# Dense gate tiles from two fp32r products with the gate values in two parts

## The chip, the cores and the metric

The kernel runs on one core of a Trainium2 chip. The metric is the device time of one execution in microseconds (us). Engines are called PE (matrix products; PEld is its weight load), DVE (vector), ACT (scalar, activations), POOL (GpSimd, here mostly the issuer of gather DMAs) and SP (the queue that issues most DMAs).

## The reference, cut to what matters

Two layers of a trunk over 512 latent tokens (and 256 context tokens in the first layer) with 1024 channels. Each layer ends in PEER retrieval: a token has 8 heads, each head picks 16 of 16384 experts by product keys, and an expert is a pair of rows of two tables u and v.

```python
top_s, pos = lax.top_k(cand, PEER_TOPK)
eidx = jnp.take_along_axis(cidx, pos, axis=-1)          # expert = i * 128 + j
gate = jax.nn.softmax(top_s, axis=-1)
act = jax.nn.gelu(jnp.einsum('nd,nhkd->nhk', hb, u_tab[eidx]).astype(F32), approximate=False)
w = (gate * act).astype(hb.dtype)
return jnp.einsum('nhk,nhkd->nd', w, v_tab[eidx])
```

So a token has 128 chosen experts (i, j), each with a gate value.

## The kernel before, in words

Tokens lie in tiles of 128. Most tiles are "dense": for them the kernel computes u times the token for all 16384 experts, with Gelu, multiplies by a 128x128 matrix of gates of each token (zero but for the chosen experts) and multiplies the product with v. Layer 0 has four dense tiles (n = 512 columns) and two gathered ones, layer 1 has three (n = 384) and one. A gathered tile fetches its rows of u and v with indirect DMAs (POOL, L667), and DVE works each row off with one 128x1024 instruction (L671, L675).

A layer's PEER has a first stage over 128 chunks of u (`u_chunk`): SP loads a chunk (`c_raw`, 512 KB), ACT casts it to fp32r (`c_hi`, L297), DVE subtracts to get the rest (`c_lo`, L298), and PE makes 24 products into `ups` (8 blocks of channels, three products each: c_hi with the high part of the tokens `opah`, c_hi with the low part `opal`, c_lo with `opah`; in layer 1 the names are `opch` and `opcl`). ACT's Gelu (`at`, L938) empties `ups`. `c_hi` and `c_lo` have two buffers, so those of a chunk wait for PE's end of the chunk two before. A second stage multiplies the gated values with v (`res`).

The gates are made beside the first stage. `select(t)` finds a tile's experts and leaves, transposed so that a partition is one of a token's 128 choices and a column a token, the row numbers -i and the gate values in `ijT` (L804), and the column numbers j as bf16 in `jT`. `build(t)` then goes over the 128 tokens, four at a time (W8), which makes 32 builds a tile, 224 in all (128 in layer 0, 96 in layer 1). For one build:

- ACT makes `o1`: per token |iota - i| (L820, four instructions of 128 columns), then Relu(1 - that) over all four (L821): a one where the row matches.
- DVE makes `oe`, a bf16 one where the column number matches (L824), and multiplies it by the gate values into `o2` (L825). `oe` lies as columns by tokens, tokens innermost; `o2` is written as tokens by columns, so DVE's writes go with a stride of 512 bytes.
- PE multiplies o1 and o2 of each token, a plain fp32 product of 128 columns (`gps`). One fp32 product shows as two MATMUL and two LDWEIGHTS records, so a build is 8 records.
- ACT copies `gps` to `stage` (L830), which goes to DRAM every fourth build.

`back` decides what is queued behind each chunk: it keeps clocks for PE, DVE and DMA from the table COST (a build is entered with 1.03 on DVE and .85 on PE), issues a share of the builds after each chunk and fills DVE with rows of the gathered tiles while its clock is behind. That table is the same before and after. Instructions on an engine run in the order in which they were issued by the framework; a wait holds up what stands behind it.

## Time and profile before

| What | Before |
|---|---|
| time, median of 3 runs | 3865.34 us (3862.36 to 3866.61) |
| the profiled execution | 3875.51 us, span 3873.7 us |
| PE, PEld busy in the span | 95%, 82% |
| DVE, ACT, POOL busy | 80%, 47%, 46% |
| mean granted clock of PE | 0.979 of 2.4 GHz |

The shares are means over stages with different limits. Builds run from 804.7 us to 3280.8 us in two stretches, about 780 to 1380 us (layer 0) and 2880 to 3290 us (layer 1). Matmul records overlap their neighbours, so the pace of PE is read from starts, not from durations.

### The profile page before, as it was taken

How to read it: one execution, taken by the hardware profiler on the slowest of the kernel's cores; microseconds unless marked ns; L12 is line 12 of the kernel's file. 1: busy time of each engine (PE TensorE's matmuls, PEld its weight loads, DVE VectorE, ACT ScalarE, POOL GpSimd, SP SyncE). 2: the span in 40 equal slices, each digit the busy share in tenths (PEclk: the TensorE clock that was granted, in tenths of full speed). 3: DMA queues.
4: the chain of work that ended last, by engine and by line, in shares of the span. 5: the costliest groups of instructions: out<-in, count | busy, mean ns of one | idle time of the engine just before them, and what ended most of it. 6: DMA issues, size and time to landing. Idle time of an engine off the chain costs nothing. (4 is left out here: it accounts for less than half of the span.)

```text
span 3873.7 us, 56946 instructions
## 1 busy us (share of the span) xinstructions
PE 3669.3 (95%) x20375; PEld 3169.8 (82%) x20375; DVE 3109.4 (80%) x6128; ACT 1839.1 (47%) x3241; POOL 1785.7 (46%) x1225
## 2 busy tenths in 40 slices
PE   7789999999999999999999899899999999999998
PEld 5567778787888778888887888789999999887877
DVE  4876899999999968877776715688999996677778
ACT  4243322377788932322224434533348999333332
POOL 4300155456556557777771203203433331577773
PEclk9899999999999999999999999899999999999999
DMA  5225589899999999989994440157989897888885
GB/s 230 87 90 202 208 320 329 309 332 357 359 347 358 371 327 357 339 321 335 336 330 139 139 135 4 66 177 266 312 296 335 322 326 272 276 312 321 320 320 198
DMA packets 377147, 1043.98 MB, mean 270 GB/s; under 512 B 32288, under 2 KB 171936, under 8 KB 346656
## 3 DMA queue, kind: packets, MB, share of 16 engines
q1 hardware_dynamic: 262960, 619.56, 44.2%
q0 software_dynamic: 113760, 420.53, 30.4%
q8 instruction: 160, 2.62, 0.3%
q14 instruction: 123, 1.01, 0.1%
q10 hardware_dynamic: 144, 0.26, 0.0%
HBM read 915.98 MB, written 124.26 MB: 269 GB/s over the span
## 5 line engine op out<-in xcount | busy, mean ns | idle before, releaser
L667 POOL DMA_INDIRECT g_row<-in_peer_u_dram,g_idx x384 | 562.7, 1465 | 670.7 <-DVE g_row L671 296.4
L667 POOL DMA_INDIRECT g_row<-in_peer_v_dram,g_idx x384 | 573.4, 1493 | 283.3 <-DVE g_acc L675 157.1
L1075 POOL TENSOR_TENSOR w<-ag,gg 128x512 f32<-128x512 f32 (+1 forms) x256 | 487.8, 1906 | 379.6 <-DVE w_lo L298 286.3
L298 DVE TENSOR_TENSOR v_lo<-v_raw,v_hi 128x1024 fp32r<-128x1024 f32 x256 | 392.4, 1533 | 286.9 <-ACT v_hi L297 286.9
L297 ACT CAST c_hi<-c_raw 128x1024 fp32r<-128x1024 f32 x304 | 318.2, 1047 | 618.4 <-PE ups L69 516.6
L297 ACT CAST v_hi<-v_raw 128x1024 fp32r<-128x1024 f32 x256 | 269.5, 1053 | 701.3 <-PE res L69 411.1
L69 PE MATMUL res<-v_hi,w_hi 128*128 128x512 f32 x1792 | 555.4, 390 | 10.3 <-ACT w_hi L297 10.2
L69 PE MATMUL res<-v_lo,w_hi 128*128 128x512 f32 x1792 | 554.6, 390 | 1.2
L69 PE MATMUL res<-v_hi,w_lo 128*128 128x512 f32 x1792 | 553.5, 389 | 0.0
L675 DVE SCALAR_TENSOR_TENSOR g_acc<-g_row,g_act,g_acc 128x1024 f32<-128x1024 f32 x381 | 520.1, 1365 | 4.4 <-DMA g_row<-in_peer_v_dram,g_idx 1.8
L298 DVE TENSOR_TENSOR c_lo<-c_raw,c_hi 128x1024 fp32r<-128x1024 f32 x304 | 372.4, 1225 | 144.7 <-ACT c_hi L297 144.2
L671 DVE SCALAR_TENSOR_TENSOR g_row<-g_row,g_h 128x1024 f32<-128x1024 f32 x384 | 471.7, 1245 | 12.6 <-DMA g_row<-in_peer_u_dram,g_idx 12.6
L69 PE MATMUL ups<-opah,c_lo 128*128 128x512 f32 x1152 | 453.8, 395 | 14.0 <-DVE c_lo L298 13.7
L69 PE MATMUL ups<-opah,c_hi 128*128 128x512 f32 x1152 | 461.6, 401 | 3.9 <-ACT c_hi L297 3.9
L69 PE MATMUL ups<-opal,c_hi 128*128 128x512 f32 x1152 | 453.2, 393 | 0.0
L69 PEld LDWEIGHTS res<-v_hi,w_hi 128*128 128x128 f32 x1792 | 336.0, 188 | 83.8 <-ACT w_hi L297 14.8
L69 PEld LDWEIGHTS res<-v_lo,w_hi 128*128 128x128 f32 x1792 | 335.9, 188 | 74.8 <-DVE v_lo L298 5.8
L69 PE MATMUL ups<-opch,c_hi 128*128 128x384 f32 x1152 | 393.5, 342 | 1.8 <-ACT c_hi L297 1.8
L69 PEld LDWEIGHTS res<-v_hi,w_lo 128*128 128x128 f32 x1792 | 335.9, 188 | 70.8 <-DVE w_lo L298 1.7
L69 PE MATMUL ups<-opch,c_lo 128*128 128x384 f32 x1152 | 388.1, 337 | 3.1 <-DVE c_lo L298 3.1
L69 PE MATMUL ups<-opcl,c_hi 128*128 128x384 f32 x1152 | 387.0, 336 | 0.0
L820 ACT ACTIVATE o<-iota,ijT 128x128 f32<-128x128 f32 x896 | 290.5, 399 | 0.0
(487 smaller groups left out, 6738.5 us busy)
## 6 DMA issues: line engine op xcount, KB each, us to landing
c_raw<-in_uT_dram SPq DMA_DIRECT2D x256, 512.0 KB, 6.5
v_raw<-in_peer_v_dram SPq DMA_DIRECT2D x128, 1024.0 KB, 6.9
G_d<-stage SPq DMA_DIRECT2D x56, 1024.0 KB, 7.9
c_raw<-in_peer_wq_dram SPq DMA_DIRECT2D x64, 512.0 KB, 4.9
gg<-G_d SPq DMA_DIRECT2D x64, 512.0 KB, 9.5
A_d<-at SPq DMA_DIRECT2D x120, 256.0 KB, 6.6
ag<-A_d SPq DMA_DIRECT2D x30, 1024.0 KB, 10.1
gg<-G_d SPq DMA_DIRECT2D x64, 384.0 KB, 7.9
```

The costliest lines, as they stand in the source:

```text
L69: self.last = self.engine.matmul(*args, **kw)
L297: copied[0] = S.copy(hi, src)
L298: return V.tensor_tensor(lo, src, hi.bitcast(F32), op=OP.subtract)
L667: G.indirect_dma_start(out=row, out_offset=None, in_=a[f"peer_{'uv'[tab]}{l}"], in_offset=bass.IndirectOffsetOnAxis(ap=idx[i][:, s:s + 1], ...
L671: V.scalar_tensor_tensor(row, row, 1.0, h, op0=OP.mult, op1=OP.mult, accum_out=w)
L675: V.scalar_tensor_tensor(acc, row, w, acc, op0=OP.mult, op1=OP.add)
L820: S.activation(o1[:, i], iota, AF.Abs, bias=tr[:, 0, n0 + i:n0 + i + 1])
L1075: G.tensor_tensor(w.rearrange("p (t m) -> p t m", m=TG), ag[:, i], gg[:, :, (c + i) % GG, :], op=OP.mult)
```

## The change

The gate values are split into a high part rounded to fp32r (kept in the third row of `ijT`) and a low part `gl`. `oe` is multiplied by each part, so `o2` becomes `o2h` and `o2l`, both fp32r, both kept as columns by tokens, which DVE writes without a stride. PE makes two fp32r products per token, o1 with o2h and o1 with o2l, added up in PSUM; it reads a token's 128 columns of o2 with a stride of 16 bytes. ACT writes |iota - i| into a tile `of` of its own and Relu of it into `o1`. The buffers change: `o1` two to one, `oe` two to one, `o2h` two, `o2l` one, `of` one.

```diff
-                S.copy(tr, pt)
+                S.copy(tr[:, :2], pt[:, :2])
                 jb = wp.tile([P, P], BF16, name="jT", bufs=2)
                 S.copy(jb, pt[:, 1])
-                chosen[t] = tr, jb
+                gl = wp.tile([P, P], F32R, name="gl", bufs=2)
+                split(tr[:, 2].bitcast(F32R), gl, pt[:, 2])
+                chosen[t] = tr, jb, (tr[:, 2], gl.bitcast(F32))
...
-                tr, jb = chosen.pop(t)
+                tr, jb, gh = chosen.pop(t)
...
-                        o1 = wp.tile([P, W8, P], F32, name="o1", bufs=2)
-                        o2 = wp.tile([P, W8, P], F32, name="o2", bufs=2)
+                        sh, nb = [P, P, W8], slice(n0, n0 + W8)
+                        o1 = wp.tile([P, W8, P], F32R, name="o1", bufs=1)
+                        o2 = [wp.tile(sh, F32R, name=f"o2{y}", bufs=b_) for y, b_ in (("h", 2), ("l", 1))]
+                        of = wp.tile([P, W8, P], F32, name="of", bufs=1)
                         for i in range(W8):
-                            S.activation(o1[:, i], iota, AF.Abs, bias=tr[:, 0, n0 + i:n0 + i + 1])
-                        S.activation(o1, o1, AF.Relu, bias=1.0, scale=-1.0)
-                        sh, nb = [P, P, W8], slice(n0, n0 + W8)
-                        oe = wp.tile(sh, BF16, name="oe", bufs=2)
+                            S.activation(of[:, i], iota, AF.Abs, bias=tr[:, 0, n0 + i:n0 + i + 1])
+                        S.activation(o1, of, AF.Relu, bias=1.0, scale=-1.0)
+                        oe = wp.tile(sh, BF16, name="oe", bufs=1)
                         V.tensor_tensor(oe, iotar, jb[:, nb].unsqueeze(1).to_broadcast(sh), op=OP.is_equal)
-                        V.tensor_tensor(o2.rearrange("p n c -> p c n"), oe, tr[:, 2, nb].unsqueeze(1).to_broadcast(sh),
-                                        op=OP.mult)
+                        for y in range(2):
+                            V.tensor_tensor(o2[y], oe, gh[y][:, nb].unsqueeze(1).to_broadcast(sh), op=OP.mult)
                         pg = pp.tile([P, W8, P], F32, name="gps", tag="misc", bufs=4)
                         for i in range(W8):
-                            PE.matmul(pg[:, i], o1[:, i], o2[:, i], start=True, stop=True)
+                            for y in range(2):
+                                PE.matmul(pg[:, i], o1[:, i], o2[y][:, :, i], start=y == 0, stop=y == 1)
```

With the single buffers the framework also issues builds in another place. Numbers at a name tell one buffer or one build from another; the rows are from layer 0, where two builds follow one chunk.

On PE, before, the two builds (10564, 10584) stand together between the last product of chunk 10526 and the first of chunk 10602:

```order
L69 MATMUL ups_10526<-opah0_1455,c_lo_10523 128x512
L69 MATMUL gps_10564<-o2_10555,o1_10554 128x128
L69 MATMUL gps_10564<-o2_10555,o1_10554 128x128 x3
L69 MATMUL gps_10584<-o2_10575,o1_10574 128x128
L69 MATMUL gps_10584<-o2_10575,o1_10574 128x128 x3
L69 MATMUL ups_10602<-opah0_1455,c_hi_10598 128x512
```

On PE, after, at a like place (the last of the eight products of build 10451, then chunk 10501, then build 10476):

```order
L69 MATMUL gps_10451<-o2l_10440,o1_10438 128x128
L69 MATMUL ups_10501<-opah0_1455,c_hi_10497 128x512
L69 MATMUL ups_10501<-opal0_1457,c_hi_10497 128x512
L69 MATMUL ups_10501<-opah0_1455,c_lo_10498 128x512
L69 MATMUL ups_10501<-opah0_1455,c_hi_10497 128x512
L69 MATMUL ups_10501<-opal0_1457,c_hi_10497 128x512
L69 MATMUL ups_10501<-opah0_1455,c_lo_10498 128x512
L69 MATMUL gps_10476<-o2h_10464,o1_10463 128x128
L69 MATMUL gps_10476<-o2l_10465,o1_10463 128x128
```

The second build of a pair has moved six products (seven in layer 1) into the next chunk; no two builds stand together any more. Before there are 43 such pairs in layer 0 and 21 in layer 1; 32 are among the first 96 builds of layer 0 and 10 among the first 66 of layer 1, and as many of these builds stand early in a chunk after.

On ACT, before, for the same pair (`at` is the Gelu of a chunk, `stage` the copy of a finished build):

```order
L297 CAST c_hi_10663<-c_raw_10661 128x1024
L938 ACTIVATE at_10551<-ups_10526 128x512
L830 COPY stage_10490<-gps_10564 128x4x128
L820 ACTIVATE o1_10634<-iota_62,ijT_9746 128x128
L830 COPY stage_10490<-gps_10584 128x4x128
```

On ACT, after, for builds 10451 (first) and 10476 (second) behind chunk 10410:

```order
L297 CAST c_hi_10566<-c_raw_10564 128x1024
L942 ACTIVATE at_10435<-ups_10410 128x512
L834 COPY stage_10317<-gps_10451 128x4x128
L825 ACTIVATE o1_10463<-of_10466 128x512
L824 ACTIVATE of_10536<-iota_62,ijT_10172 128x128
L824 ACTIVATE of_10536<-iota_62,ijT_10172 128x128 x3
L834 COPY stage_10317<-gps_10476 128x4x128
```

Before, the `o1` of both builds was made ahead of these rows; after, the Relu that makes the second build's `o1` stands behind the copy of the first build.

On DVE, before, the two multiplications of a pair stand behind one `c_lo`:

```order
L298 TENSOR_TENSOR c_lo_10599<-c_raw_10596,c_hi_10598 128x1024
L825 TENSOR_TENSOR o2_10555<-oe_10561,ijT_9746 128x128x4
L825 TENSOR_TENSOR o2_10575<-oe_10581,ijT_9746 128x128x4
```

On DVE, after, from the `c_lo` of chunk 10570 on:

```order
L298 TENSOR_TENSOR c_lo_10567<-c_raw_10564,c_hi_10566 128x1024
L829 TENSOR_TENSOR o2l_10465<-oe_10472,gl_10176 128x512
L753 MAX topd_10384<-candd_10387 128x8
L827 TENSOR_TENSOR oe_10542<-iotar_2702,jT_10174 128x512
L754 MAX_INDEX posd_10385<-topd_10384,candd_10387 128x8
L829 TENSOR_TENSOR o2h_10534<-oe_10542,ijT_10172 128x512
L755 MATCH_REPLACE c2d_10623<-topd_10384,candd_10387 128x96
L675 SCALAR_TENSOR_TENSOR g_acc_86<-g_row_10650,g_act_2681,g_acc_86 128x1024
L829 TENSOR_TENSOR o2l_10535<-oe_10542,gl_10176 128x512
```

Each build now has two multiplications on DVE, and the one that writes `o2l` waits for PE's products of the build before; in its place on the queue it mostly stands behind a `c_lo`.

## Rows read from the trace of the kernel before

**Rows 1.** Windows: stretch, length, then busy PE, PEld, DVE, ACT, POOL (instructions), clock, DMA, GB/s.
```profile
780.00:1260.00 480.00, 459.49 (x2368) 386.75 (x2366) 474.97 (x863) 380.90 (x750) 286.64 (x175) 0.99 0.96 351
1260.00:1380.00 120.00, 110.87 (x604) 93.53 (x605) 107.33 (x165) 102.70 (x215) 65.85 (x45) 1.00 0.99 372
2880.00:3180.00 300.00, 298.57 (x1903) 297.63 (x1901) 286.21 (x570) 268.58 (x527) 108.15 (x76) 1.00 0.90 322
3180.00:3290.00 110.00, 102.45 (x656) 98.21 (x655) 78.22 (x92) 104.66 (x224) 23.48 (x16) 1.00 0.77 278
```
**Rows 2.** Waits in 780 to 1260 us: who waited for whom, total us, times, longest.
```profile
ACT c_hi L297 <- PE ups L69: 67.0, 40, 4.4
...
PEld gps L69 <- ACT o L821: 14.8, 10, 2.9
```
**Rows 3.** DVE's groups in 780 to 1380 us: busy us, mean ns | idle before.
```profile
L825 DVE TENSOR_TENSOR o<-oe,ijT 128x512 f32<-128x512 bf16 x128 | 137.0, 1086 | 2.1 <-PE gps L69 2.1
L298 DVE TENSOR_TENSOR c_lo<-c_raw,c_hi 128x1024 fp32r<-128x1024 f32 x81 | 98.7, 1218 | 8.1 <-ACT c_hi L297 8.1
L824 DVE TENSOR_TENSOR oe<-iotar,jT 128x512 bf16<-128x512 bf16 x128 | 51.2, 416 | 0.0
```
**Rows 4.** Chain of work in 3030 to 3090 us: start us, us, what.
```profile
3036.20 0.89 PE gps L69 x8
3037.09 4.17 PE ups L69 x24
```
**Rows 5.** DVE over the whole span: 512 fp32 elements of two SBUF tiles into fp32r.
```profile
L298 DVE TENSOR_TENSOR w_lo<-w,w_hi 128x512 fp32r<-128x512 f32 x128 | 87.3, 682 | 0.0
```
**Rows 6.** Line L825 alone by stretch: length, busy us (instructions), clock, DMA, GB/s.
```profile
780.00:1260.00 480.00, 102.66 (x96) 0.99 0.96 351
...
2880.00:3180.00 300.00, 70.55 (x66) 1.00 0.90 322
```
**Rows 7.** PE's timeline from 2350.3 us: start us, us, what.
```profile
2350.29 1.45 PE L69 MATMUL po<-gkv,apT 128*128 128x64 f32 x12
2351.58 1.11 PE L69 MATMUL mlps<-vx,kw 128*128 128x129 f32 x8
```
**Rows 8.** Weight loads over the whole span, by form.
```profile
L69 PEld LDWEIGHTS gps<-o,o 128*128 128x128 f32 x1792 | 223.5, 191 | 55.4 <-ACT o L821 39.1 <-ACT o L820 3.3 <-issue 3.0
L69 PEld LDWEIGHTS ups<-opah,c_hi 128*128 128x128 f32 x1152 | 218.7, 190 | 48.6 <-ACT c_hi L297 7.3
...
L69 PEld LDWEIGHTS modp<-modw,scT 128*2 128x2 f32 x1024 | 27.4, 94 | 19.6 <-issue 10.2 <-DMA modw<-in_mod_w_dram 3.6 <-DVE sib L721 0.8
```
**Rows 9.** PE's timeline in layer 1's projection, fp32r products of 256 columns.
```profile
2292.66 0.28 PE L69 MATMUL tps<-t_hi,opbh 128*128 128x256 f32 x1
2292.78 0.28 PE L69 MATMUL tps<-t_lo,opbh 128*128 128x256 f32 x1
```
**Rows 10.** PE's timeline around one build in layer 0.
```profile
1006.21 0.39 PE L69 MATMUL ups<-opal,c_hi 128*128 128x512 f32 x1
1006.44 0.40 PE L69 MATMUL ups<-opah,c_lo 128*128 128x512 f32 x1
1006.67 1.06 PE L69 MATMUL gps<-o,o 128*128 128x128 f32 x8
1007.48 0.48 PE L69 MATMUL ups<-opah,c_hi 128*128 128x512 f32 x1
```
**Rows 11.** ACT's timeline behind the same chunk.
```profile
1006.69 1.03 ACT L297 CAST c_hi<-c_raw 128x1024 fp32r<-128x1024 f32 x1
1007.63 0.59 ACT L938 ACTIVATE at<-ups 128x512 f32<-128x512 f32 x1
1008.11 1.06 ACT L830 COPY stage<-gps 128x512 f32<-128x512 f32 x1
1008.97 1.27 ACT L820 ACTIVATE o<-iota,ijT 128x128 f32<-128x128 f32 x4
1010.27 0.63 ACT L821 ACTIVATE o<-o 128x512 f32<-128x512 f32 x1
```

## The prediction

> **What bounds the kernel now.** I read the busy times by stretch first, since the page's means mix stages. In the first part of layer 0's builds (780 to 1260 us) DVE is busy 474.97 of 480 us, PE 459.49 and ACT 380.90 [rows 1]: DVE has 5 us left and PE 20.5. The next 120 us, where builds come three to a chunk, have no engine full: PE 110.87, DVE 107.33, ACT 102.70. In layer 1, from 2880 to 3180 us, PE is busy 298.57 of 300 us and DVE 286.21; then ACT takes over (104.66 of 110 us) while DVE falls to 78.22 [rows 1]. Then the waits: in the full stretch of layer 0, PE's idle time before builds is mostly put down to ACT's Relu (14.8 us), and ACT itself waits 67 us for PE to give the chunk buffers back [rows 2]. DVE waits hardly at all: 2.1 us before o2, 8.1 us before c_lo over 600 us [rows 3]. So in layer 0 DVE works without a pause and PE just keeps up; in layer 1 the chain of work is PE alone, 4.17 us for a chunk and 0.89 us for a build [rows 4], with DVE 14 us short of full.
>
> **DVE, the term that counts.** One strided multiplication of 1086 ns goes [rows 3], two unstrided ones come. The nearest row is w_lo: 512 elements of two SBUF tiles, at least one of them fp32, into fp32r, 682 ns [rows 5]. A build then costs 2 x 0.682 - 1.086 = +0.278 us on DVE. Bounds: the new form is not in the trace. If the stride was not what made the old one slow, both cost 1.086, +1.09 us a build; if both ran like the bf16 comparison oe, 416 ns [rows 3], the build saves 0.25 us. I take 0.682, because there an fp32 operand is read as here, while oe is bf16 throughout.
> Layer 0, full stretch: 96 builds [rows 6] x 0.278 = 26.7 us on an engine with 5 us of idle time. I put +27 there, since the idle time did not close before either. The other 32 builds add 8.9 us where DVE has 12.7 us to spare [rows 1]: nothing. If that cover fails, it costs those 8.9 us.
> Layer 1: 66 builds [rows 6] x 0.278 = 18.3 us, DVE to 304.6 of 300 us: it becomes the bound by 4.6 us. The last 30 builds fall where DVE has 32 us to spare: nothing.
> The splitting of the gates is once a tile, seven times, each three instructions of 128 columns where one of 384 is cut to 256: an estimate of 0.3 us each on DVE (less than oe's 0.416 for four times the columns), 1 us on the path.
>
> **PE.** A build was 8 records of fp32, and is 8 of fp32r: two products for a token instead of the two passes of one. What can a product of 128 columns cost? Twelve records of po with only 64 columns take 2351.58 - 2350.29 = 1.29 us, 0.108 us each [rows 7]; eight of gps with 128 columns take 0.89, 0.111 each [rows 4]. Half the columns do not make it faster, so the weight load of 128 columns sets the pace, not the stream. That load is the same for fp32r: 190 ns in ups against 191 in gps, where one of 2 columns takes 94 [rows 8]. And the new products load o1 twice per token, as before. So a record stays at 0.108 at the least; the nearest fp32r row, 256 columns, is 0.12 apart [rows 9], the upper end if the strided read is free. I take 0.117 x 8 = 0.94, +0.05 us a build: hidden behind DVE in layer 0, 66 x 0.05 = 3 us in layer 1. If the stride costs at most the time of a second column each, the stream of 128 columns lasts like one of 256, which is again the 0.12. The bound above: four column times each, as long as the 512 column products, 0.23 us [rows 10], 1.84 a build, +0.95.
> The Trainium skill speaks against this strided read: SBUF — State Buffer, "Door 1" with its note on cachelines, has 16-byte lines, full rate from two hits in a line on, and a penalty for each access that goes to a new line; here every column is a new line. No row of this case shows a strided moving operand, so by that rule the sum lies between my 0.94 and the 1.84 above; it is the second rival's ground.
> The Trainium skill has a rule on the other side too: TensorE: Matmul & The Clock Gate, "Back-to-back issue gap", gives about 81 ns for a pair of weight load and product of 128 columns. The trace disagrees for four-byte weights: 0.108 us even with 64 columns [rows 7]. By that page of the Trainium skill a build would be 0.65 us, an estimate, and layer 1's stretch would lose 16 us of PE work, none of which counts while DVE has 304.6 us to do in it.
>
> **Order and single buffers.** The waits added: Relu into o1 and the multiplication into o2l now wait for PE's previous build. Behind the first stand ACT's next Abs, c_hi and Gelu; behind the second DVE's gather rows and c_lo. Where one build follows a chunk, the previous build is 0.89 + 4.17 us or more ahead and o2l stands behind a c_lo of 1.22 us [rows 3, 4], so nothing is late. Where two follow, the second has moved six products into the next chunk, and its Relu stands behind c_hi, Gelu and the copy of the first. Counted from the chunk's end (by starts, as records overlap): c_hi to copy 1.42, copy to next 0.86, Relu 0.63 [rows 11], so o1 is there 2.9 us after. PE is there after 0.81 for the first build and 6 x 0.23 = 1.4 [rows 10], 2.2 us after. PE stands 0.7 us per pair: 32 pairs in layer 0's full stretch, 22 us; 10 in layer 1's, 7 us (there 7 products of 0.174 against a shorter Gelu, the same 0.7). In layer 0 most of this lies beside the time that PE lacks DVE anyway (27 us more stretch, and 20.5 us idle before); I charge 3 us. In layer 1 PE is the bound, so all 7 count. In the tails ACT's instructions are the same in number and size, 0. Between 0 and all 29 us is possible here.
>
> **Sum.** Layer 0: 27 + 3 + 1 = 31. Layer 1: PE pace 3, pairs 7, and 2 for the chunks in which DVE's 4.6 us do not lie beside these = 12. Together +43 us. What follows (the second stages) is on PE at its pace and gives nothing back. The profiled execution was 3875.51 us for a span of 3873.7, 10 us over the median; the rows carry over as differences, so I add to the median: 3865 + 43 = 3908 us. Own range of this case: with the pairs free and the layer 1 terms at zero, +25; with all pair stalls in full and layer 0's terms added, +70: 3890 to 3935.
>
> **Rivals.**
> 1. *PE pays for the strided read or for the short fp32r product.* For it: nothing in the trace has fp32r under 256 columns or a strided moving operand, and all fp32r products of this kernel are 256 wide or wider. Against it: the weight load leaves room for two column times. At four, PE gains 0.95 us a build: layer 0's full stretch 459.5 + 91 = 551 us of PE work in 480, and its 20 us of other idle time, about +90; tail 110.9 + 30 = 141, +21; layer 1 298.6 + 63, +62; tail 102.5 + 29 = 131, +21. About +195, 4060 us. At three, half of it, about 3960.
> 2. *The other side: DVE gets cheaper.* Place: the multiplications of layer 0's full stretch. If the unstrided form reads bf16 beside a gate that it holds for long runs and goes at oe's 416 ns, DVE saves 0.25 x 96 = 24 us there, and PE's 20.5 us of idle time can go less the 22 us of pair stalls; it decides from 543 ns an instruction down (two then equal the old one). Best case 3865 - 15 = 3850 us. Against it: fp32 rows with two tensors are all at one pace, 1218 for 1024 and 682 for 512 [rows 3, 5].
> 3. *Single buffers lock DVE and PE to each other.* If DVE reaches o2l before PE is through the earlier build, it stands with its gather rows behind it, up to a chunk. PE at 0.89 a build would have to be late by more than the 1.22 us of c_lo; at 0.5 us more for each of the 162 builds in the full stretches, +81 on top, 3990 us.
> 4. *Nothing measurable:* DVE's extra 27 us lies in time that PE's and ACT's mutual waits take anyway. DVE's 99% speaks against it. 3868 us.
>
> **Chances.** Forecast 0.66, rival 1 0.12, rival 2 0.07, rival 3 0.08, rival 4 0.07. The range of 3866 to 3990 takes in the forecast, rival 4 at its upper half, rival 3 and the milder half of rival 1. A measurement here can tell about 0.2%, 8 us, from no change. Faster: rival 2, 0.07. Within: rival 4 and a little of the first, 0.09. Slower: 0.84.
>
> **What would show it.** The two multiplications at about 0.68 us each; DVE full in layer 0 until about 1290 us; gps records 0.11 to 0.12 us apart; PE's wait before builds early in a chunk named after ACT's Relu, some 0.7 us; layer 0's chunks stretched, the second stages as long as before. I am wrong if the multiplications take under 0.55 us or about 1.09, or if gps records stand 0.2 us apart.

## The result and the profile after

The changed kernel takes 3967.51 us (median; 3959.18 to 3970.16) against 3865.98 us (3862.36 to 3877.92) beside it: 101.5 us slower, ratio 1.0253, 95% interval 1.0226 to 1.028. The forecast was 43 us slower. The sign was right, the size was not: the loss is more than double.

The four stretches of [rows 1], after:

```profile
780.00:1260.00 480.00, 441.64 (x2145) 364.19 (x2144) 461.64 (x885) 349.79 (x674) 234.69 (x159) 0.96 0.90 320
1260.00:1380.00 120.00, 106.71 (x555) 86.47 (x554) 113.71 (x200) 104.43 (x213) 44.64 (x41) 0.99 0.93 333
2880.00:3180.00 300.00, 287.60 (x1737) 282.02 (x1736) 279.42 (x660) 221.91 (x416) 87.25 (x69) 0.99 0.85 297
3180.00:3290.00 110.00, 104.18 (x650) 101.26 (x649) 104.65 (x180) 99.47 (x198) 37.82 (x27) 1.00 0.90 312
```

No engine is full any more. In the first stretch DVE has fallen from 474.97 to 461.64 us although it has more to do, PE from 459.49 to 441.64, and the granted clock from 0.99 to 0.96. In layer 1 PE, 298.57 of 300 us before, is at 287.60. DVE's groups in 780 to 1380 us, as in [rows 3]:

```profile
L298 DVE TENSOR_TENSOR c_lo<-c_raw,c_hi 128x1024 fp32r<-128x1024 f32 x74 | 90.5, 1223 | 19.9 <-ACT c_hi L297 19.7
...
L829 DVE TENSOR_TENSOR o2l<-oe,gl 128x512 fp32r<-128x512 bf16 x116 | 79.4, 685 | 0.5 <-PE gps L69 0.5
L829 DVE TENSOR_TENSOR o2h<-oe,ijT 128x512 fp32r<-128x512 bf16 x116 | 79.1, 682 | 0.6
```

The two multiplications cost what the forecast took, 682 and 685 ns. DVE's idle time stands before c_lo (19.9 us, 8.1 before), in waits for ACT's cast, which in turn waits for PE. The waits of 780 to 1260 us, as in [rows 2]:

```profile
ACT c_hi L297 <- PE ups L69: 90.3, 49, 4.4
...
PEld gps L69 <- ACT o L825: 30.7, 32, 1.9
ACT stage L834 <- PE gps L69: 25.8, 20, 4.3
PEld gps L69 <- DVE o2l L829: 24.9, 20, 3.6
PE gps L69 <- DVE o2l L829: 21.0, 15, 3.4
PE gps L69 <- ACT o L825: 16.6, 31, 1.5
```

PE waits for ACT's Relu as forecast, but also 21 us for o2l, of which the forecast said that nothing is late. What one such place looks like on PE's timeline:

```profile
928.04 0.39 PE L69 MATMUL ups<-opah,c_lo 128*128 128x512 f32 x1
928.88 0.36 PE L69 MATMUL gps<-o2h,o 128*128 128x128 f32 x1 [0.45 <-ACT o L825]
932.44 0.48 PE L69 MATMUL gps<-o2l,o 128*128 128x128 f32 x1 [3.20 <-DVE o2l L829]
932.73 0.40 PE L69 MATMUL gps<-o2h,o 128*128 128x128 f32 x1
932.94 0.40 PE L69 MATMUL gps<-o2l,o 128*128 128x128 f32 x1
...
934.53 0.63 PE L69 MATMUL ups<-opal,c_hi 128*128 128x512 f32 x1
934.96 0.63 PE L69 MATMUL ups<-opah,c_lo 128*128 128x512 f32 x1
```

Read the starts: after the wait the products of the build are 0.21 us apart, not 0.12, and those of ups 0.43, not the 0.23 of [rows 10]. The granted clock from 931.2 to 937.8 us is 0.50, the lower of its two levels, 1.2 GHz:

```profile
931.20:937.80 6.60, 5.36 (x16) 4.58 (x17) 6.60 (x12) 2.77 (x6) 5.09 (x2) 0.50 0.88 326
```

Two sums are used below for every run: over the two spans from some chunks before the first build to the last chunk of each layer (752 to 1475 and 2900 to 3417 us here; 751 to 1415 and 2839 to 3323 before), the time at the lower clock, from the trace's clock records, and PE's idle time, from its gaps. Before they are 6.8 and 39.9 us, after 47.7 and 85.1. The two spans together are 93.4 us longer. Where they grow is read from starts: whatever the distance of two starts has over the distance of such products at full clock goes to a wait (if the record before it ended more than 0.15 us earlier), else to the lower clock, else to pace. By this count 59 of the 93 us stand at waits, 17 are products at the lower clock and 17 are pace.

The clock falls ten times in the two spans. Eight of the falls begin during a wait for o2l of 1.2 to 3.4 us or within 1.7 us after it, and seven of these eight waits begin 32 us or more after the last stretch at the lower clock. So the wait comes first. Where it comes from shows at the first of all waits for o2l, 1.18 us before the product of 819.86 us, when the clock had been at its upper level for 321 us. DVE works without a pause there, but three other instructions stand between the c_lo and the o2l that PE needs:

```profile
815.43 1.22 DVE L298 TENSOR_TENSOR c_lo<-c_raw,c_hi 128x1024 fp32r<-128x1024 f32 x1
816.57 1.28 DVE L675 SCALAR_TENSOR_TENSOR g_acc<-g_row,g_act,g_acc 128x1024 f32<-128x1024 f32 x1
817.76 0.25 DVE L757 MAX8 topd<-c2d 128x8 f32<-128x96 f32 x1
817.93 1.27 DVE L675 SCALAR_TENSOR_TENSOR g_acc<-g_row,g_act,g_acc 128x1024 f32<-128x1024 f32 x1
819.12 0.68 DVE L829 TENSOR_TENSOR o2l<-oe,gl 128x512 fp32r<-128x512 bf16 x1
```

In 124 of the 224 builds a c_lo stands between a build's oe and its o2l on DVE. In the kernel before one stands between oe and o2 in 55.

### The profile page after: what moved, and what is told of

Its sections match the earlier page's. It is cut to its first block, busy times and chain, and to the rows that moved or that the text cites. A ratio compares the mean times of both kernels' runs of the same rounds, so it can differ in the third digit from the quotient of the medians.

```text
span 3967.1 us, 57044 instructions
## 1 busy us (share of the span) xinstructions
PE 3720.1 (94%) x20375; PEld 3196.2 (81%) x20375; DVE 3183.6 (80%) x6359; ACT 1861.9 (47%) x3248; POOL 1716.9 (43%) x1225
## 3 DMA queue, kind: packets, MB, share of 16 engines
q1 hardware_dynamic: 262960, 619.56, 43.5%
## 5 line engine op out<-in xcount | busy, mean ns | idle before, releaser
L667 POOL DMA_INDIRECT g_row<-in_peer_u_dram,g_idx x384 | 519.6, 1353 | 756.1 <-DVE g_row L671 391.4
L667 POOL DMA_INDIRECT g_row<-in_peer_v_dram,g_idx x384 | 548.1, 1427 | 347.4 <-DVE g_acc L675 213.5
L824 ACT ACTIVATE of<-iota,ijT 128x128 f32<-128x128 f32 x896 | 287.3, 391 | 6.8
```

The lines of the kernel that those rows point to most:

```text
L667: G.indirect_dma_start(out=row, out_offset=None, in_=a[f"peer_{'uv'[tab]}{l}"], in_offset=bass.IndirectOffsetOnAxis(ap=idx[i][:, s:s + 1], ...
L824: S.activation(of[:, i], iota, AF.Abs, bias=tr[:, 0, n0 + i:n0 + i + 1])
```

## The experiments

The first theory was that DVE's added time and the single buffers lock DVE and PE to each other (rival 3 of the prediction, milder). Its rivals: DVE's time alone; PE's new products, by pace or by clock. Times are against the kernel before, run beside each.

| Run | us over before | ratio, 95% interval | low clock, us | PE idle, us |
|---|---|---|---|---|
| the change | +101.5 | 1.0226 to 1.028 | 47.7 | 85.1 |
| before, single buffers | +13.0 | 1.0023 to 1.0048 | 0.0 | 43.4 |
| before, more DVE | +22.3 | 1.0041 to 1.0083 | 10.2 | 51.2 |
| before, both of these | +28.6 | 1.006 to 1.0093 | 3.4 | 49.8 |
| change, two buffers of o1 | +114.6 | 1.0271 to 1.0318 | 95.5 | 94.3 |
| change, all doubled | +81.2 | 1.0192 to 1.0235 | 85.4 | 61.0 |
| before, fewer raw buffers | +8.0 | 1.0011 to 1.0032 | 13.6 | 41.2 |
| change, half the low part | +64.1 | 1.0153 to 1.0187 | 37.5 | 67.5 |
| change, planner told | +138.2 | 1.0338 to 1.0382 | 17.0 | 61.3 |
| change, high products first | +79.6 | 1.0186 to 1.022 | 34.1 | 79.6 |
| before, unstrided write | +152.1 | 1.0375 to 1.0422 | 0.0 | 1.9 |
| before, fp32r products | +47.4 | 1.0104 to 1.014 | 64.8 | 60.2 |
| before, all three | +134.5 | 1.0326 to 1.0365 | 81.9 | 128.6 |
| before, fp32r, 256 columns | 0.0 | 0.9989 to 1.0008 | 6.8 | 31.9 |
| change, 256 columns | +43.5 | 1.0098 to 1.0134 | 6.8 | 46.4 |
| before, tokens outermost | -2.6 | 0.9983 to 1.0003 | 10.2 | 34.6 |
| before, one instruction a token | -27.3 | 0.9917 to 0.995 | 0.0 | 25.5 |
| change, high part alone | -37.9 | 0.9879 to 0.9923 | 6.8 | 79.0 |
| the same, two buffers | -48.4 | 0.9861 to 0.9894 | 23.9 | 69.1 |

### The two costs that the forecast priced, each alone

Before, with one buffer each (Abs goes to a tile of its own):

```diff
-                        o1 = wp.tile([P, W8, P], F32, name="o1", bufs=2)
-                        o2 = wp.tile([P, W8, P], F32, name="o2", bufs=2)
+                        o1 = wp.tile([P, W8, P], F32, name="o1", bufs=1)
+                        of = wp.tile([P, W8, P], F32, name="of", bufs=1)
+                        o2 = wp.tile([P, W8, P], F32, name="o2", bufs=1)
...
-                        oe = wp.tile(sh, BF16, name="oe", bufs=2)
+                        oe = wp.tile(sh, BF16, name="oe", bufs=1)
```

> The kernel before, its arithmetic untouched, with one buffer each of o1, oe and o2 and Abs into a tile of its own. Theory W: PE's waits before builds rise as in the changed kernel, 3866 + 40 to 60 = about 3905 to 3925, with more stretches at the lower granted clock. Theory D: no DVE or PE work is added, so within 10 us of 3866.

Before, with one more DVE instruction a build (284 ns by its row):

```diff
+                        xd = wp.tile([P, P], F32, name="xd", bufs=1)
+                        V.tensor_tensor(xd, iota, tr[:, 2], op=OP.mult)
```

> The kernel before with one more DVE instruction per build (128 fp32 columns into a tile that nobody reads, about 0.28 us). Theory D: DVE is full in layer 0, so 96 x 0.28 = 27 us there and about 5 us in layer 1, about 3898. Theory W: the work lies in time that PE's and ACT's waits take anyway, below 3880.

Both edits in one kernel:

> The kernel before with both of the edits that were tried apart: one buffer each of o1, oe and o2 (alone +13 us), and one more VectorE instruction of 284 ns in each build (alone +22 us). If the two add, the run takes some 35 us more than before, about 3902 us. If they act on each other (a full VectorE can't run ahead of TensorE where its tiles have one buffer, so each waits for the other), it takes 55 us or more, 3920 us and up, with TensorE's idle time before the gates' product above 25 us in the first layer's middle stretch and its clock low for more than the 3.4 us of before there.

13.0 and 22.3 us apart, 28.6 us together: with fp32 products the two add to somewhat less than their sum. So the locking theory fails for the kernel before, and the clock falls hardly more than before (0.0, 10.2 and 3.4 us against 6.8). The forecast had 29 us for DVE (27 and 2 in the two layers) and 10 for the buffers. The added instruction is somewhat short of the change's: DVE's records overlap too, and by starts it adds 0.20 us to a build, the change 0.28 (0.335 + 0.601 + 0.602 against 0.335 + 0.923). Some 65 to 73 us of the 101.5 are somewhere else. Set against this run with both edits, the change's two spans are 66 us longer: 46 at waits, 19 at the lower clock and 1 in pace.

### Buffers in the changed kernel

```diff
-                        o1 = wp.tile([P, W8, P], F32R, name="o1", bufs=1)
+                        o1 = wp.tile([P, W8, P], F32R, name="o1", bufs=2)
...
-                            S.activation(of[:, i], iota, AF.Abs, bias=tr[:, 0, n0 + i:n0 + i + 1])
-                        S.activation(o1, of, AF.Relu, bias=1.0, scale=-1.0)
+                            S.activation(o1[:, i], iota, AF.Abs, bias=tr[:, 0, n0 + i:n0 + i + 1])
+                        S.activation(o1, o1.bitcast(F32), AF.Relu, bias=1.0, scale=-1.0)
```

> The changed kernel with Abs written straight into o1 (whole numbers up to 127, which fp32r holds) and two buffers of o1 instead of of and one o1; DVE and PE work as in the changed kernel. Theory W (waits from single buffers, Relu queued behind the copy of the build before): PE's wait for ACT's Relu (129 us over the span in the changed kernel) falls below 60, the time by 25 to 45 us, to about 3925 to 3940. Theory D (DVE's 0.28 us a build is the cost): time within 10 us of the changed kernel's 3967.

It is 13 us slower than the change, each against its own kernel before. The idle time before gps over the whole kernel, by what ended it (total us, times), of the change:

```profile
  ACT o L825: 129.1, 160
  DVE o2l L829: 68.7, 79
```

The same of this run:

```profile
  DVE o2l L828: 187.8, 156
...
  ACT o L823: 18.7, 21
```

This view adds up the idle times of PE and of PEld, so that one wait can count twice; the recorded expectations count in the same way. PE's own records have 43.1 us (73 times) for ACT's Relu and 30.1 us (35 times) for o2l in the change, and 24.7 us (31 times) for the Relu before. In the run with two buffers of o1 the wait for ACT goes and one for o2l takes its place, and the time at the lower clock doubles. Taking one wait away paid nothing.

Two buffers of o1, oe, o2h and o2l, for which the raw chunk and weight buffers go from (4, 5) to (3, 4); beside it, before with that last edit alone:

> The changed kernel with two buffers each of o1 (in place), oe, o2h and o2l; to make room, the raw chunks of u have three buffers in layer 0 and four in layer 1 instead of four and five. Theory W (single buffers make PE wait, and PE's clock falls): PE's idle time in layer 0's full stretch falls from 37 us back to about 20, the lower clock from 37 us to under 10, and the time to the DVE term (22 us as measured by one more DVE instruction) and the pace of PE (0.075 us a build, 10 to 17 us): 3869 + 32 to 45 = about 3900 to 3915. Theory D (two multiplications a build are too much, wherever they stand): above 3940.

> The kernel before with three and four raw chunk buffers instead of four and five: the control for the kernel above. Both theories: within 8 us of 3869; if not, that much is taken off the other.

+81.2 us, or some 73 less the 8 us of the fewer raw buffers. Doubling everything takes 24 us of idle time away but leaves 85 us of low clock: the single buffers are not the main cause. DVE makes o2l right behind o2h in this run and PE waits only 3.7 us for it, yet the clock falls 15 times, now mostly at waits for o2h and for ACT.

### DVE's load and the order in the changed kernel

The low part for half the columns (o2l is one lasting tile; the other columns keep a fixed content):

```diff
+                        V.tensor_tensor(o2[0], oe, gh[0][:, nb].unsqueeze(1).to_broadcast(sh), op=OP.mult)
+                        V.tensor_tensor(lowp[:, :P // 2], oe[:, :P // 2], gh[1][:, nb].unsqueeze(1).to_broadcast(hc),
+                                        op=OP.mult)
```

> The changed kernel with the low part o2l made for half of its columns only (the other columns keep a fixed content, so the low part of these gates is left out); o2l has one buffer and TensorE's 8 products of a build are unchanged. VectorE does about 0.31 us less in each build. If VectorE's time in the builds sets the end, through the waits that it makes, 160 builds of layer 0 and most of layer 1's 64 give back 50 to 70 us: 3900 to 3915 us, and the stretches of lower clock get fewer. If the time went to TensorE's pace and to the order of the waits alone, it gives back 15 us or less: 3950 us or more.

It gives back 37 us, between both forecasts. The instruction fell from 684 to 418 ns, 0.27 us, or 60 us over 224 builds, so DVE's time, with the waits and the low clock that go with it, counts with about 0.6 of its length. A build costs DVE 0.416 + 0.684 + 0.418 = 1.52 us then, as much as before (1.50), and still the run is 64 us slower than before.

The planner's table with DVE's time of a build set to 1.8 in place of 1.03:

> The changed kernel with the planner's DVE cost of a build at 1.8 instead of 1.03, so that fewer rows of the gathered tiles are worked off beside the builds and more in the second stage, where DVE has room. Theory D: DVE is relieved, o2l comes in time, 3967 less 30 to 50, about 3920 to 3935. Theory W: o2l still waits for the build before and stands behind c_lo, so within 12 us of 3967.

The two spans get 44 us shorter than after's, to 1196.2 us, but the run is 37 us slower: the last gathered row is fetched at 3925.6 us, where after it is 3878.1. My reading, not tested, is that the planner leaves rows of the gathered tiles for the second stage, where nothing hides them. It tells nothing about the cause sought.

The 4 high products ahead of the 4 low ones:

```diff
-                        for i in range(W8):
-                            for y in range(2):
-                                PE.matmul(pg[:, i], o1[:, i], o2[y][:, :, i], start=y == 0, stop=y == 1)
+                        for y in range(2):
+                            for i in range(W8):
+                                PE.matmul(pg[:, i], o1[:, i], o2[y][:, :, i], start=y + i == 0, stop=y * i == W8 - 1)
```

> The changed kernel with the 8 products of a build in another order: first the 4 with the high part, then the 4 with the low part, all added in the same place. TensorE then waits for o2l 0.35 us later in a build, with three more products done. If the second wait inside a build is what costs (68.7 us before gps, and the low clock behind it), the wait for o2l shrinks by a third or more and the run gives back 20 to 40 us: 3925 to 3945 us. If o2l is late by much more than 0.35 us each time because VectorE is full, at most 10 us: 3955 us or more.

22 us come back, the lower end of what the first forecast gave; the wait for o2l before gps falls from 68.7 to 50.9 us, a quarter where it had a third, and the low clock from 47.7 to 34.1. DVE's order is that of the change but for half a dozen instructions of 6359, so this run moves the wait alone. The place of the wait matters, but it is not the whole.

### PE's part

The strided read needed a measure of its own: before, in fp32, with o2 written without and read with a stride.

```diff
-                        o2 = wp.tile([P, W8, P], F32, name="o2", bufs=2)
+                        o2 = wp.tile([P, P, W8], F32, name="o2", bufs=2)
...
-                        V.tensor_tensor(o2.rearrange("p n c -> p c n"), oe, tr[:, 2, nb].unsqueeze(1).to_broadcast(sh),
+                        V.tensor_tensor(o2, oe, tr[:, 2, nb].unsqueeze(1).to_broadcast(sh),
...
-                            PE.matmul(pg[:, i], o1[:, i], o2[:, i], start=True, stop=True)
+                            PE.matmul(pg[:, i], o1[:, i], o2[:, :, i], start=True, stop=True)
```

> The kernel before with o2 kept as columns by tokens, written by DVE without a stride and read by PE with 16 bytes of stride, fp32 and double buffers as before. DVE's multiplication falls from 1.09 to about 0.68 us. Theory D: layer 0 loses DVE work of 0.40 x 96 = 38 us, of which PE's 20 us of idle time bound the gain, about 3848. If the strided read costs a fp32 product anything, gps records stand further apart than 0.111 us: at 0.118 it is +0.05 us a build. Theory W alone: no gain over 5 us.

DVE's multiplication falls to 689 ns, but PE is full, at full clock. The window of the first stretch:

```profile
780.00:1260.00 480.00, 479.52 (x2107) 407.91 (x2106) 407.82 (x781) 344.14 (x661) 217.62 (x157) 1.00 0.90 315
```

And two builds together on its PE timeline, between products of ups:

```profile
1003.50 0.40 PE L69 MATMUL ups<-opah,c_lo 128*128 128x512 f32 x1
1003.73 3.80 PE L69 MATMUL gps<-o,o 128*128 128x128 f32 x16
1007.17 0.59 PE L69 MATMUL ups<-opah,c_hi 128*128 128x512 f32 x1
1007.60 0.39 PE L69 MATMUL ups<-opal,c_hi 128*128 128x512 f32 x1
```

From 1003.50 to 1007.60 us less two products of ups (0.227 each) a build adds 1.82 us; by the same count, which serves for every build below, the median before is 0.902. So a stride of 16 bytes doubles the time of a build in fp32. The Trainium skill, SBUF — State Buffer, "Door 1" with its note on cachelines, has a penalty for each access that goes to a new line. This run agrees, at a factor of two. In the change the same stride costs 0.118 against 0.112 us a product without it (next run). My reading, not tested: the one-pass product streams half as long, and the pace that the weight load sets (about 0.11 us, [rows 7, 8]) covers most of the doubled stream.

Then PE's part of the change alone: fp32r, each product taken twice, contiguous read, two buffers, DVE as before.

```diff
+                        o1 = wp.tile([P, W8, P], F32R, name="o1", bufs=2)
+                        o2 = wp.tile([P, W8, P], F32R, name="o2", bufs=2)
...
+                        S.activation(o1, o1.bitcast(F32), AF.Relu, bias=1.0, scale=-1.0)
...
+                            for y in range(2):
+                                PE.matmul(pg[:, i], o1[:, i], o2[:, i], start=y == 0, stop=y == 1)
```

> The kernel before with TensorE's part of the change alone: o1 and o2 typed as fp32r, and each of the 4 products of a build taken twice in one pass and added (so the gates come out doubled, and without their low part). Two buffers each, VectorE's work, the strided write of o2 and the contiguous read as before. If TensorE's part costs only its pace (+0.05 us on each of 224 builds), the run is 10 to 15 us slower than before, 3880 to 3885 us, and the low clock stays at some 7 us in the four stretches. If the shorter products also let the clock fall behind the waits that are there in any case, the low clock takes 30 us or more and the run is 30 us or more slower, 3900 us and up.

+47.4 us, although a build adds no more on PE (898 ns, median, against 902 before) and DVE's multiplication is the same (1090 ns). PE's order is the same but for 18 builds that stand 2 to 12 products earlier. DVE's order is not: with the shorter products the framework puts a c_lo between a build's oe and its o2 in 126 builds, where before it is 55. The other difference is the clock, 0.96 in the first stretch; the second window is one of its falls:

```profile
780.00:1260.00 480.00, 452.27 (x2252) 380.55 (x2253) 456.23 (x831) 361.38 (x704) 268.64 (x165) 0.96 0.91 332
925.60:932.40 6.80, 6.80 (x21) 5.64 (x22) 6.76 (x11) 4.47 (x12) 3.49 (x3) 0.50 0.88 295
```

PE's timeline of this run around that second window:

```profile
922.75 0.40 PE L69 MATMUL ups<-opah,c_lo 128*128 128x512 f32 x1
922.99 1.00 PE L69 MATMUL gps<-o,o 128*128 128x128 f32 x8
925.46 1.85 PE L69 MATMUL gps<-o,o 128*128 128x128 f32 x8 [1.48 <-DVE o L825]
927.12 0.73 PE L69 MATMUL ups<-opah,c_hi 128*128 128x512 f32 x1
927.65 0.63 PE L69 MATMUL ups<-opal,c_hi 128*128 128x512 f32 x1
```

PE's timeline of the kernel before, at a wait of the same length:

```profile
951.58 0.39 PE L69 MATMUL ups<-opah,c_lo 128*128 128x512 f32 x1
953.43 1.13 PE L69 MATMUL gps<-o,o 128*128 128x128 f32 x8 [1.46 <-DVE o L825]
954.31 0.48 PE L69 MATMUL ups<-opah,c_hi 128*128 128x512 f32 x1
954.63 0.40 PE L69 MATMUL ups<-opal,c_hi 128*128 128x512 f32 x1
```

The window behind that wait, also of the kernel before:

```profile
953.60:960.40 6.80, 6.80 (x39) 5.92 (x39) 6.76 (x14) 6.74 (x15) 3.11 (x3) 1.00 1.03 411
```

In fp32r the wait stands between two builds and the clock is at 1.2 GHz behind it (ups 0.43 to 0.53 us apart); in fp32 the clock stays at 2.4 GHz (1.00). The places are not alike in all: before, a chunk's products and not a build stand ahead of the wait. So I count. Take PE's waits of 1.4 us and more in the two spans, and call a wait followed by a fall if the lower clock begins during the wait or within 5 us behind it. Here there are 19 such waits, 11 followed by a fall; before there are 7, 2 followed. Over all runs, of the waits of 1.4 to 2 us, 4 of 24 are followed in the eight kernels with fp32 products and 32 of 69 in the eight with eight fp32r products of 128 columns; of longer waits, 7 of 9 and 46 of 51. So the fp32r kernels have more long waits, and more of their middling ones are followed by a fall. Of the 44 us by which the two spans are longer here, 21 stand at waits and 25 are products at the lower clock, and 2 come back in pace.

All three parts (single buffers, more DVE, fp32r products twice) on the kernel before:

> The kernel before with one buffer each of o1, oe and o2, one more VectorE instruction in each build (both as before: together +29 us), and the fp32r products taken twice (the gates come out doubled, without their low part). All three costs of the change are in it, only that TensorE waits for one VectorE tile in a build and not for two in turn. If the three add, 3910 to 3920 us. If the loss comes from the products' form together with the waits (the clock), 3940 us and up with more than 30 us of low clock in the four stretches. If it stays under 3920 us, the rest of the +101 us lies in what this kernel lacks: the second wait, for o2l, between the first and the second product of a token.

+134.5 us, where the parts alone make 28.6 + 47.4 = 76. With fp32r products the waits do act on each other: idle time is 128.6 us. The same two edits with fp32 products gave 49.8. Here too the order on DVE is another one: a c_lo stands between oe and o2 in 131 builds, in that run in 85.

The test of the cause: the same number of products and weight loads, but each product takes 256 columns, two tokens at a time. First in the kernel with PE's part alone, then in the changed kernel, where the 256 columns lie side by side:

```diff
-                                PE.matmul(pg[:, i], o1[:, i], o2[:, i], start=y == 0, stop=y == 1)
+                                h = i // 2 * 2
+                                PE.matmul(pg[:, h:h + 2], o1[:, i], o2[:, h:h + 2], start=y + i == h, stop=y + i == h + 2)
```
```diff
-                                PE.matmul(pg[:, i], o1[:, i], o2[y][:, :, i], start=y == 0, stop=y == 1)
+                                h, c = i // 2 * 2, i % 2 * 64
+                                PE.matmul(pg[:, h:h + 2], o1[:, i], o2[y][:, c:c + 64], start=y + i == h, stop=y + i == h + 2)
```

> The kernel of the run with TensorE's part alone (before, with o1 and o2 in fp32r and 8 one-pass products a build), but each product takes 256 columns (the o2 of two tokens) and not 128; the gates come out as sums of two tokens, without their low part. The rows of before have 256-column fp32r products 0.12 us apart, so the pace of a build stays near 0.95 us, only the array streams twice as long in it. If the short one-pass products are what lets TensorE's clock fall behind waits, the low clock goes from 65 us in the four stretches back under 20 us and the run from +47 to +10 to +25 us, 3878 to 3893 us. If the fall has another cause in the fp32r form, the low clock stays above 45 us and the run at +47 us or more, since the pace is a little longer.

> The changed kernel with each of its 8 products of a build taken over 256 columns that lie side by side in o2h or o2l (half of its columns for all four tokens) in place of 128 columns read with the stride; the gates are not those of the reference. VectorE, ScalarE, the buffers and the number of products and weight loads are as changed, the pace of a product as well (0.118 us against 0.12). If the clock behind the short products costs part of the change's +101 us, the low clock goes from 48 us under 15 us and the run gives back 20 to 50 us, 3918 to 3948 us. If the clock has no part, it stays at 3960 us or more.

PE's part alone goes from +47.4 us to 0.0 with products of twice the columns, though a build now adds 961 ns. The window of its first stretch has its clock back:

```profile
780.00:1260.00 480.00, 461.94 (x2369) 390.25 (x2368) 476.68 (x864) 384.17 (x754) 290.47 (x175) 1.00 0.96 352
```

On its PE timeline a wait of 1.55 us leaves the pace of ups at 0.23:

```profile
947.85 0.39 PE L69 MATMUL ups<-opal,c_hi 128*128 128x512 f32 x1
949.78 1.19 PE L69 MATMUL gps<-o,o 128*128 128x256 f32 x8 [1.55 <-DVE posd L754]
950.81 0.39 PE L69 MATMUL ups<-opah,c_lo 128*128 128x512 f32 x1
951.04 0.40 PE L69 MATMUL ups<-opah,c_hi 128*128 128x512 f32 x1
```

But the columns are not all that changes. The framework's order on DVE goes back as well: a c_lo stands between oe and o2 in 70 builds (126 with 128 columns, 55 before), and PE has 5 waits of 1.4 us and more, 2 of them followed by a fall. Of the 41 us that the two spans lose against the run with 128 columns, 29 are at waits and 25 at the lower clock, and 13 come back in pace. What this run shows is that the short product, with what the framework makes of it, costs the 47 us; how much of it is the product and how much the order it does not show.

The changed kernel goes from +101.5 to +43.5 us. Its idle time before gps over the whole kernel, to be set against the 129.1 and 68.7 above:

```profile
  ACT o L825: 81.1, 131
...
  DVE o2l L829: 1.0, 4
```

Windows of two of its stretches:

```profile
780.00:1260.00 480.00, 450.57 (x2222) 367.40 (x2221) 470.74 (x909) 363.20 (x700) 268.22 (x163) 0.99 0.92 327
...
2880.00:3180.00 300.00, 297.70 (x1841) 294.11 (x1840) 291.76 (x659) 247.74 (x472) 103.00 (x72) 1.00 0.88 312
```

The lower clock is all but gone (47.7 to 6.8 us), and so is the wait for o2l (68.7 to 1.0 us); DVE and, in layer 1, PE are nearly full again. The expectation took VectorE's work to be as in the change. Its order is not: a c_lo stands between oe and o2l in 59 builds and not in 124, and from the end of o2h to the start of o2l it is 0.79 us on average and not 1.90. At the build that was shown above, o2l now comes right behind c_lo, and PE does not wait for it:

```profile
817.33 1.21 DVE L298 TENSOR_TENSOR c_lo<-c_raw,c_hi 128x1024 fp32r<-128x1024 f32 x1
818.46 0.68 DVE L829 TENSOR_TENSOR o2l<-oe,gl 128x512 fp32r<-128x512 bf16 x1
819.07 1.27 DVE L675 SCALAR_TENSOR_TENSOR g_acc<-g_row,g_act,g_acc 128x1024 f32<-128x1024 f32 x1
```

In neither run was the clock low in the 50 us before this build, so a low clock cannot have made that wait. The two spans lose 52.9 us: 48 at waits and 18 at the lower clock, and 13 come back in pace. A build without a wait adds 965 ns in layer 0, as after (964).

### Faster kernels

Two edits of the kernel before, in fp32. First, iotar, oe and o2 all as tokens by columns:

```diff
-                        sh, nb = [P, P, W8], slice(n0, n0 + W8)
+                        sh, nb = [P, W8, P], slice(n0, n0 + W8)
...
+                        V.tensor_tensor(oe, iotar, jb[:, nb].unsqueeze(2).to_broadcast(sh), op=OP.is_equal)
+                        V.tensor_tensor(o2, oe, tr[:, 2, nb].unsqueeze(2).to_broadcast(sh), op=OP.mult)
```

> The kernel before, in fp32, with iotar, oe and o2 all as tokens by columns: VectorE writes o2 without a stride and TensorE reads it without one. If the strided write is what makes the product 1086 ns, it falls to about 690 ns and TensorE's build stays at 0.90 us: VectorE loses 0.40 us a build, and the time falls to 3820 to 3840 us, no further, since TensorE is idle for only 40 us in the four stretches. If the gate's broadcast along the innermost dimension costs what the stride did, o2 stays near 1.09 us, oe may cost up to 0.69 us in place of 0.42, and the time is 3865 to 3885 us.

No change: o2 falls to 685 ns, but oe rises to 679 in place of 416, and the 0.14 us left (0.05 by starts) do not show. Second, one instruction a token in place of oe and o2:

```diff
+                        for i in range(W8):
+                            V.tensor_scalar(o2[:, i], iota, tr[:, 1, n0 + i:n0 + i + 1], tr[:, 2, n0 + i:n0 + i + 1],
+                                            op0=OP.is_equal, op1=OP.mult)
```

> The kernel before, in fp32, with oe and o2 replaced by one VectorE instruction for each token (compare with the token's index, then multiply with its gate, both as scalars of the partition), 4 in a build, written without a stride. At the 284 ns of one 128-column fp32 instruction a build costs VectorE 1.14 us in place of 1.50. If VectorE's share is what bounds the kernel's middle stretches, the time falls by 20 to 40 us, to 3825 to 3845 us; if TensorE bounds them it stays within 10 us of before.

27.3 us faster than before, as expected by the theory that DVE bounds layer 0, although an instruction takes 364 ns there and not 284. By starts the four take 1.03 us and the two before 1.26. This kernel computes the gates in full and beats both others.

The changed kernel with the high part alone, and that with two buffers of o1, oe and o2h:

> The changed kernel without the low part: one multiplication and one fp32r product for a token, single buffers of o1 and oe as in the change (it leaves out the low part of the gates). DVE has 1.10 us a build (before 1.50, changed 1.78), PE 4 records of 0.118 us. Theory D: DVE is no longer full in layer 0 and PE saves 0.4 us a build in layer 1: 3869 less 30 to 50, about 3820 to 3840. Theory W (waits for the one o1 alone): above 3860, PE waiting for ACT's Relu as in the changed kernel (25 us in the full stretches).

> The changed kernel with the high part alone (the low part of the gates is left out, so they are rounded to fp32r) and two buffers each of o1, oe and o2h; the run with the high part alone and single buffers was 38 us under before, with TensorE waiting 94 us in layer 0's stretch for ScalarE's Relu. If single buffers make these waits, the wait halves and the run comes to 3795 to 3820 us. If the short products let the clock fall at the waits that are left, as in the kernel before with TensorE's part alone, the low clock rises above 30 us and the run stays at 3830 us or more.

37.9 and 48.4 us faster than before, at the price of gates rounded to fp32r. The low part is thus what makes the change a loss. The second lies at the upper end of its range: the idle time for ACT before gps (PE and PEld) falls from 187.4 to 140.6 us, not by half, and the low clock is 23.9 us. These are short fp32r products too, four a build, and with single buffers the low clock stays at 6.8 us beside 79 us of idle time, so such products do not always let the clock fall.

## Why the prediction was wrong

- **DVE**: right in size. 682 and 685 ns were taken as 682. The added time alone cost 22.3 us where 29 were forecast, with an instruction of 0.20 us by starts for the change's 0.28.
- **PE's pace**: right. Products of the change are 0.118 us apart (taken: 0.117), a build takes 964 and 951 ns in the two layers, +0.06 us against the +0.05 forecast. With 256 columns the same +0.06 costs nothing in layer 0 and 3.1 us in the span of layer 1, where "66 x 0.05 = 3 us" was forecast.
- **Order and single buffers**: the wait for ACT's Relu came where it was put (31 times, 16.6 us on PE in the first stretch, before 6 times and 9.5 us; forecast 32 times and 22 us). Single buffers alone cost 13.0 us, forecast 3 + 7. "Nothing is late" for o2l is wrong: PE's own records wait 35 times and 30.1 us for it. The prediction put one c_lo ahead of o2l; in the change rows of the gathered tiles stand there as well, and eight of the ten falls of the clock stand at these waits.
- **The step that failed** is the one on PE, that a build costs "+0.05 us a build: hidden behind DVE in layer 0, 66 x 0.05 = 3 us in layer 1". It priced the product by the distance of records and left everything else as it was: the clock of [rows 1], 0.99 and 1.00, and the time at which DVE's tiles come ("nothing is late"). In the runs the short one-pass product, at an unchanged pace, comes with longer waits for DVE and ACT, and the clock falls behind them. Put alone into the kernel before it costs 47.4 us, 21 at waits and 25 at the lower clock in the two spans. In the change 58.0 us go when the products take 256 columns and o2l stands earlier on DVE.
- **The sum** came out right only for a kernel without these waits: with 256 columns the change is at +43.5 us, and its two spans are 33 us longer in layer 0 and 7.4 in layer 1; forecast 43, 31 and 12. Part of this is luck, since that run has another order on DVE than the change, and since single buffers and more DVE in fp32 cost 28.6 us where the forecast had 39 for the two. The lower bound of +25 does not follow from the prediction's terms either (27 + 1 are 28).
- **Signs**: none of the three signs of being wrong came. Of what would show the forecast, "DVE full in layer 0" failed, with 461.64 of 480 us.
- **Rivals**: the first one named the short fp32r product, but as a longer record; the record was as forecast, and that the time is near this rival's 3960 us is chance. (The prediction calls the strided read the second rival's ground; it is the first's.) The third, DVE and PE locked by single buffers, is not it: DVE waits for PE before o2l only once in the first stretch, 0.5 us, and doubled buffers leave +81.2 us. The Trainium skill, TensorE: Matmul & The Clock Gate, "Why this matters for your kernels", names idle gaps between bursts as what lowers the clock. The trace agrees that each fall stands at a wait, 10 of 10 in the change and 13 of 13 with PE's part alone.

Open: how the 47.4 and the 58.0 us divide between the short product itself and the order that the framework gives DVE with it. The counts of waits speak for both, but no run keeps the order and changes the number of columns alone. Also open is why four fp32r products a build lose little clock and eight much. The 256-column run of the change also reads without a stride, so the stride's own part in the clock was not tried apart.

## What to carry to other kernels

Price a product on PE twice: by the distance of its records, and by what happens at the waits around it, the clock included. An edit of one engine's instructions can move another engine's: compare the order on every engine before calling an experiment a change of one thing. Look at the granted clock by windows of each stretch, and ask of each fall which wait stands before it and what made that wait. And where an engine is full before a change and has more to do after it, but is no longer full, look for a new wait: here DVE fell from 474.97 to 461.64 us of 480.

## What was not expected of the hardware

- With the moving operand (o2) read with a stride of 16 bytes, a build in fp32 takes 1.82 against 0.90 us, at full clock.
- In fp32r the same stride costs 0.118 against 0.112 us a product of 128 columns.
- With the column number broadcast along the innermost dimension the bf16 comparison takes 679 ns, as much as the multiplication with fp32 output; with it broadcast along the outer one it takes 416.
- With 256 columns in place of 128 in the same number of fp32r products, and the order on DVE that came with it, a kernel is 45.7 us faster (3915.62 to 3869.88).
- Of PE's waits of 1.4 to 2 us, 4 of 24 are followed by the lower clock in kernels with fp32 products and 32 of 69 in those with eight 128-column fp32r products a build; above 2 us it is 7 of 9 and 46 of 51.
